# A hybrid RWKV-7 and Conformer layer on one core: the convolution's LayerNorm in two steps, two gate pairs kept in SBUF, and an order for the first squares

## The chip, the core and the metric

The kernel runs on one core of a Trainium2 chip. The time is that of one execution on the device in microseconds, the median of several. The core has five engines, each of which works through its own list of instructions in a fixed order and waits by semaphores for the others: TensorE (PE) for matrix products, VectorE (DVE) and ScalarE (ACT) for elementwise work, GpSimd (POOL), and SyncE (SP), which issues most transfers. PE loads weights (PEld) beside a running product. Products land in PSUM, which has eight banks; everything else is kept in SBUF in named tiles with a fixed number of buffers.

## What is computed

One layer of a decoder over a prompt of 2048 tokens (width 1024) and eight sample tokens. The convolution branch and the merge, which the change touches, are in the reference:

```python
h = rms_norm(x, norm_pre_g)
proj = jnp.einsum('btd,dn->btn', h, w_in)
...
u = u_in[..., :D_CONV] * jax.nn.sigmoid(u_in[..., D_CONV:])
c = lax.conv_general_dilated(buf, conv_w[:, None, :], ...) + conv_b      # 31 taps per channel
cm = jnp.mean(cf, axis=-1, keepdims=True)
cv = jnp.mean(jnp.square(cf - cm), axis=-1, keepdims=True)
cn = (cf - cm) * lax.rsqrt(cv + LN_EPS) * ln_c_g + ln_c_b
o_c = jax.nn.silu(cn) * jax.nn.silu(z_c)
branch_c = o_c @ w_branch_c
merged = jax.nn.sigmoid(g_r) * branch_r + jax.nn.sigmoid(g_c) * branch_c
y = x + rms_norm(merged @ w_out, norm_post_g)
```

The other branch is the RWKV-7 recurrence over 16 heads, done in chunks of 64 tokens, which needs a triangular solve per chunk.

## The kernel before

The prompt is cut into four blocks of 512 tokens; everything is kept transposed, channels on the partitions and tokens along the row. Each product of `gemm` makes 128 output channels of a block from 8 tiles of the input with three passes (the high part of both factors, and the two mixed terms), so 24 matmuls of 512 columns. In block 0 and in the merges of block 2, where the sample tokens ride along, a product takes two banks and twice as many matmuls of half the width. The products rotate through three PSUM banks, `pg`.

A block's loop goes over eight units j (two heads each). In each, `unit_b(j)` runs the recurrence's scan and `unit_a(j + 1)` prepares the next unit, of which the solve is a long chain of small DVE operations (lines 600 to 611); `unit_in(j + 2)` makes four products. Behind them come the fill steps of a table, one string for each j: `u` makes a channel tile of the gated linear unit (`glu`), whose 31 taps then run on DVE in small portions (`pull`), a digit makes a pair of output gates (`gate`), `n` is the LayerNorm over the 512 channels (`conv_norm`), `z` and `Z` multiply two channel tiles each with the gate of the convolution (`conv_gate`). Then `conv_split`, the next block's first products, eight merges (`merge`, two products each) and the output product (`stage_out`).

`conv_norm` adds the four channel tiles, sums over the partitions with a product with a constant matrix (`stat` with `avg_c`, line 767), subtracts, squares, sums the squares the same way (line 776), and scales. `gate` stores its sigmoids in DRAM (line 1010, issued by ACT) and `merge` loads the two rows that it needs (lines 1026 and 1027, issued by SP), both through the tag `x`, which has two buffers. `tmp` has four buffers and serves the norm, the gates of the convolution, and `unit_a`. `stage_first` normalizes the first block: it squares eight tiles of the prompt, adds and sums them, and beside it makes the sample rows' norm (`rms`).

The order on each engine is made at build time by a scheduler that goes by the order in which instructions are traced and by a model of when their inputs are ready. `later(n)` lets what it holds count as n instructions later; `behind` and `issue_after` place instructions on their engine's list behind a given one, without a wait for its end.

Of the kernel before, what the change touches and what calls it, by code (L numbers as in the profile page):

```python
# [15 lines left out]
RJ = 3  # L16
GE, HPO, HPA = 4, 0, 0
LI = 1000
LN = 200
HP = 550  # L20
HPW, HPS, HPG, HPU, HPZ = HP, HP, HP, HP, HP
LN_EXP_SET = 6
# [4 lines left out]
def rwkv7_conformer_step(  # L27
# [6 lines left out]
    nc = tc.nc  # L34
# [264 lines left out]
        return tiles  # L299

    FT, MTP, GTP, GM = 6, 6, 6, (3, 6)
    FILL0 = ("u0", "u1", "u2", "u3", "4n", "5", "6", "7zZ")
    FILL1 = ("0", "1", "2n", "z", "Z", "3", "4", "567")
    FILL2 = ("", "", "0n", "z", "Z", "1", "", "234567")
    UT = 2
    PARK = 2
    DW = {SB - 1: (2, 1, 0, 1, 0, 1, 0, 0), SB: (0, 0, 1, 0, 1, 0, 1, 1)}
    PASSES = ((0, 0), (0, 1), (1, 0))

    def gemm(specs):  # L310


        views = []
        for src, key, rhs, w2 in specs:
            ws = wload(src, key)
            v = View()
            if w2:
                outs = [(pgt()[:, 0:PW], slice(0, PW)), (pgt()[:, 0:w2], slice(PW, PW + w2))]
                v.parts = [(o[:, 0:HB], slice(i * HB, i * HB + HB)) for i, (o, _) in enumerate(outs)]
                v.s = [o[:, HB:PW] for o, sl in outs if sl.stop - sl.start == PW]  # L320
            else:
                outs = [(pgt(), slice(0, BS))]
                v.parts = outs
            n = 4 * len(ws)
            for o, sl in outs:
                for kt in range(n):
                    for pi, (wp, ap) in enumerate(PASSES):
                        mm(o, ws[kt // 4][:, wp, kt % 4, :], rhs(kt, ap)[:, sl],
                           start=(kt == 0 and pi == 0), stop=(kt == n - 1 and pi == 2))
            views.append(v)  # L330
        return views

# [57 lines left out]
    def stage_first():  # L390

        n1 = NS + 1
        xts = [new([128, 2, BS], tag) for tag in ("x", "x", "orr", "orr")]
        xts = [xts[kt // 2][:, kt % 2] for kt in range(KT)]
        for kt in range(KT):
            nc.sync.dma_start(out=xts[kt], in_=x_cols[kt, :, 0:BS])
        xs = new([128, D], "orr")
        nc.sync.dma_start(out=xs[0:NS], in_=x_sample[:, 0, :])
        nc.sync.dma_start(out=xs[NS:n1], in_=x_prompt[0, T - 1:T, :])
        gb = new([128, D], "orr")  # L400
        nc.sync.dma_start(out=gb[0:n1], in_=norm_pre_g[0:1, :].to_broadcast([n1, D]))
        sh = new([128, D], "orr")
        nc.sync.dma_start(out=sh[0:NS], in_=state_shift[0])
        rstd = rms(xs, n1, "orr", [128, D])
        h9 = new([128, D], "orr")
        stt(h9[0:n1], xs[0:n1], rstd[0:n1], gb[0:n1], ALU.mult, ALU.mult)
        with later(LI):
            nc.scalar.dma_start(out=nshift_s[0], in_=h9[0:NS])
            nc.scalar.dma_start(out=nshift_p[0], in_=h9[NS:n1])
        ps = pa()  # L410
        psv = ps[:, 0:KT * 2 * NS].rearrange("p (k i s) -> p k i s", k=KT, i=2)
        for kt in range(KT):
            for i, src in enumerate((h9, sh)):
                nc.tensor.transpose(out=psv[:, kt, i, :], in_=src[0:NS, kt * 128:kt * 128 + 128],
                                    identity=ident[0:NS, 0:NS])
        rb = new([128, BS], "tmp")
        for kt in range(KT):
            sq = rb if kt == 0 else new([128, BS], "tmp")
            act(sq, xts[kt], AF.Square)
            if kt:  # L420
                tt(rb, rb, sq, ALU.add)
        rsqrt(rb, stat(pyt, avg_c, rb), eps_rms, scale=float(DC) / D)
        ht = [new([128, 2, WX], "ht", F32R) for _ in range(KT)]
        for kt in range(KT):
            stt(xts[kt], xts[kt], pv("npre", kt), rb, ALU.mult, ALU.mult)
            split(wide(True, ht[kt][:, 0]), wide(True, ht[kt][:, 1]), two(True, xts[kt]))
            hv = ht[kt].rearrange("p h (i t) -> p h i t", i=2)[:, :, :, HB:PW]
            split(hv[:, 0], hv[:, 1], psv[:, kt])
        return ht
# [330 lines left out]
        return acc  # L760

    def conv_norm(b, cs):
        sm = new([128, BS], "tmp")
        tt(sm, cs[0], cs[1], ALU.add)
        for ct in range(2, CT):
            tt(sm, sm, cs[ct], ALU.add)
        ps = stat(pgt, avg_c, sm)
        for ct in range(CT):
            tt(cs[ct], cs[ct], ps, ALU.subtract)
        sm = new([128, BS], "tmp")  # L770
        act(sm, cs[0], AF.Square)
        for ct in range(1, CT):
            sq = new([128, BS], "tmp")
            act(sq, cs[ct], AF.Square)
            tt(sm, sm, sq, ALU.add)
        ps = stat(pgt, avg_c, sm)
        rs = new([128, BS], "tmp")
        rsqrt(rs, ps, eps_ln)
        for ct in range(CT):
            mul(cs[ct], cs[ct], rs)  # L780
            s1 = new([128, BS], "tmp")
            sigmoid(s1, cs[ct], nscale=nlng[:, ct:ct + 1], nbias=nlnb[:, ct:ct + 1])
            act(cs[ct], cs[ct], AF.Identity, scale=pv("lng", ct), bias=pv("lnb", ct))
            mul(cs[ct], cs[ct], s1)

    def conv_gate(b, ht, cs, c0):
        for i, z in enumerate(gemm([hspec(b, ht, N_SHIFT + 2 * DC + (c0 + i) * 128) for i in range(2)])):
            ct = c0 + i
            s2 = new([128, BS], "tmp")
            with tc.high_priority(HPZ):  # L790
                sigmoid_v(s2, z)
                for ps, sl in z.parts:
                    mul(s2[:, sl], s2[:, sl], ps)
                if b == 0:
                    vcp(sconv[:, 2 * CT + ct, :], z.s[0])
            mul(cs[ct], cs[ct], s2)

    def conv_split(b, cs):
        wd = b == SB
# [195 lines left out]
    G0 = N_SHIFT + 3 * DC  # L995
    gates = [[dram.tile([128, 2, BS], F32, name=f"gate{b}_{i}") for i in range(KT)] for b in range(NB)]

    def gate(b, ht, i0):

        vs = gemm([hspec(b, ht, G0 + (i0 + i) * 128) for i in range(2)])  # L1000
# [6 lines left out]
                    vcp(gate_s[:, i0 + i, :], v.s[0])  # L1007
        act(s, s, AF.Ln, bias=1.0)
        act(s, s, AF.Exp, scale=-1.0)
        nc.scalar.dma_start(out=gates[b][i0 // 2], in_=s)  # L1010

    def merge_prep(b, orr):
        if b == SB:
# [5 lines left out]
    def merge(b, m, orr, oc):  # L1019
# [1 line left out]
        w2 = HB if wd else None  # L1021
        br, bcv = gemm([(w_branch_r[m], ("br", m), lambda kt, part: orr[kt][:, part, :], w2),
                        (w_branch_c[m], ("bc", m), lambda kt, part: oc[kt][part], w2)])
        sc = new([128, 2, BS], "x")
        s, c = sc[:, 0], sc[:, 1]
        nc.sync.dma_start(out=s, in_=gates[b][m // 2][:, m % 2])
        nc.sync.dma_start(out=c, in_=gates[b][(KT + m) // 2][:, m % 2])
        for t, v in ((s, br), (c, bcv)):
            for ps, sl in v.parts:
                mul(t[:, sl], t[:, sl], ps)  # L1030
# [100 lines left out]
    def fill(b, ht, cs, what):  # L1131
# [3 lines left out]
        elif what == "n":  # L1135
            while taps:
                pull(1)
            with later(LN):
                conv_norm(b, cs)
        elif what in "zZ":  # L1140
            conv_gate(b, ht, cs, 2 * (what == "Z"))
        else:
            gate(b, ht, 2 * int(what))
# [129 lines left out]
```

## Time and profile before

| | us |
|---|---|
| three runs | 2832.56, 2832.91, 2835.99 |
| median | 2832.91 |
| profiled execution | 2830.14 |
| its span | 2828.4 |
| PE busy | 2680.2 |
| DVE busy | 1965.0 |
| ACT busy | 1318.7 |
| stores of gates, 512 KB each | 32 |
| loads of gates, 256 KB each | 64 |

Rows of a timeline give the start, the duration, the engine, the line, the operation, what it writes and reads with the tile's name, and the count of equal instructions that were drawn together. Brackets hold the time for which the engine stood idle before, and what ended that. Line numbers are often those of a helper: 101 is an operation on two tiles, 107 one with a scalar besides, 95 an activation, 113 a matmul.

### The profile page before, as it was taken

How to read it: one execution, taken by the hardware profiler on the slowest of the kernel's cores; microseconds unless marked ns; L12 is line 12 of the kernel's file. 1: busy time of each engine (PE TensorE's matmuls, PEld its weight loads, DVE VectorE, ACT ScalarE, POOL GpSimd, SP SyncE). 2: the span in 40 equal slices, each digit the busy share in tenths (PEclk: the TensorE clock that was granted, in tenths of full speed). 3: DMA queues.
4: the chain of work that ended last, by engine and by line, in shares of the span. 5: the costliest groups of instructions: out<-in, count | busy, mean ns of one | idle time of the engine just before them, and what ended most of it. 6: DMA issues, size and time to landing. Idle time of an engine off the chain costs nothing.

```text
span 2828.4 us, 55917 instructions
## 1 busy us (share of the span) xinstructions
PE 2680.2 (95%) x22800; PEld 2129.1 (75%) x22800; DVE 1965.0 (69%) x4560; ACT 1318.7 (47%) x2783; POOL 16.1 (1%) x61
## 2 busy tenths in 40 slices
PE   6999898999999989999999998999999997999988
PEld 6888887878877767777887766777797765777777
DVE  5789898677877667667568667676665767765522
ACT  5555556662344464555113556555312455545511
POOL 0000000000000000000000000000000000000000
PEclk9999999999999999999999999999999998999999
DMA  5555754547964334254665335344475422332474
GB/s 197 202 172 189 209 179 137 182 160 249 316 240 136 105 122 136 100 168 160 215 239 202 106 103 151 116 138 162 160 237 205 156 88 71 108 117 98 135 275 161
DMA packets 153107, 466.91 MB, mean 165 GB/s; under 512 B 19281, under 2 KB 24642, under 8 KB 152843
## 3 DMA queue, kind: packets, MB, share of 16 engines
q1 hardware_dynamic: 145745, 437.55, 46.3%
q10 hardware_dynamic: 7106, 25.79, 2.5%
q8 instruction: 179, 2.93, 0.4%
q14 instruction: 77, 0.63, 0.1%
HBM read 350.41 MB, written 113.35 MB: 164 GB/s over the span
## 4 chain that ended last, share of the span: by engine, by line
PE 53%; DVE 29%; ACT 13%; issue 3%; DMA 2%; SPq 0%; POOL 0%; DVEq 0%; ACTq 0%; POOLq 0%
PE pg L113 34%; PE pa L113 7%; DVE gd L101 5%; DVE zr L605 5%; PE pc L113 4%; PE py L113 4%; DVE zr L107 3%; DVE et L107 3%; ACT sc L95 2%; PE pb L113 2%; DVE raw L107 2%; ACT zbuf L95 2%; ACT xv L95 1%; DVE w L101 1%; ACT tmp L95 1%
## 5 line engine op out<-in xcount | busy, mean ns | idle before, releaser
L113 PE MATMUL pg<-ht,w 128*128 128x512 f32 (+1 forms) x7200 | 1518.6, 362 | 15.1 <-DVE sraw L110 5.3
L113 PEld LDWEIGHTS pg<-ht,w 128*128 128x128 f32 x7200 | 1163.2, 189 | 255.5 <-issue 59.8
L107 DVE SCALAR_TENSOR_TENSOR et<-u,cw,et 128x512 f32<-128x512 f32 x480 | 359.4, 749 | 6.7
L95 ACT ACTIVATE raw<-pg,omm 128x512 f32<-128x512 f32 (+1 forms) x155 | 92.9, 602 | 208.9 <-PE pg L113 201.4
L95 ACT ACTIVATE tmp<-tmp 128x512 f32<-128x512 f32 (+1 forms) x305 | 185.0, 625 | 9.0 <-DVE tmp L526 3.2
L101 DVE TENSOR_TENSOR gd<-zr,gp 128x8 f32<-128x8 f32 (+14 forms) x480 | 179.7, 374 | 11.7
L113 PE MATMUL pg<-orr,w 128*128 128x512 f32 (+2 forms) x960 | 185.0, 349 | 0.0
L605 DVE TENSOR_REDUCE zr<-gd 128x2 f32<-128x8 f32 (+14 forms) x480 | 176.6, 368 | 11.7
L113 PEld LDWEIGHTS pg<-orr,w 128*128 128x128 f32 x960 | 155.2, 188 | 25.1
L95 ACT ACTIVATE w<-wraw 128x512 fp32r<-128x512 f32 x162 | 101.3, 627 | 117.8 <-PE pg L113 75.4
L698 DVE TENSOR_SCALAR xs<-pc,dk 128x64 f32<-128x64 f32 x224 | 63.5, 284 | 111.6 <-PE pc L113 109.3
L95 ACT ACTIVATE sc<-pa 64x256 f32<-64x256 f32 (+1 forms) x192 | 72.9, 380 | 136.4 <-PE pb L113 133.1
L101 DVE TENSOR_TENSOR w<-wraw,w 128x512 fp32r<-128x512 f32 x162 | 111.0, 687 | 32.2 <-ACT w L95 31.5
L107 DVE SCALAR_TENSOR_TENSOR raw<-pg,prm,raw 128x511 f32<-128x511 f32 (+1 forms) x185 | 104.3, 574 | 29.9 <-ACT raw L95 29.3
L107 DVE SCALAR_TENSOR_TENSOR zr<-zr,sub 128x5 f32<-128x5 f32 (+7 forms) x512 | 115.7, 226 | 13.3
L95 ACT ACTIVATE gd<-sc 32x128 f32<-32x128 f32 x256 | 78.4, 306 | 92.2 <-DVE sc L101 89.6
L101 DVE TENSOR_TENSOR x<-x,pg 128x512 f32<-128x512 f32 (+1 forms) x80 | 46.2, 578 | 94.6 <-PE pg L113 56.5
L113 PE MATMUL pa<-ar,bk 64*64 64x128 f32 x2048 | 105.7, 285 | 5.6 <-DVE sc L101 3.2
L113 PEld LDWEIGHTS pa<-ar,bk 64*64 64x64 f32 x2048 | 81.3, 136 | 39.2 <-DVE bk L101 15.2
L101 DVE TENSOR_TENSOR sc<-pa,maskw 128x512 f32<-128x512 f32 x128 | 82.7, 685 | 30.8 <-PE pa L113 30.7
L101 DVE TENSOR_TENSOR keep<-pa,raw 128x512 f32<-128x512 f32 x32 | 22.1, 692 | 113.9 <-PE pa L113 113.9
L113 PE MATMUL pg<-xv,w 128*128 128x512 f32 (+2 forms) x320 | 89.8, 354 | 8.8 <-DVE x L101 8.8
(360 smaller groups left out, 3654.3 us busy)
## 6 DMA issues: line engine op xcount, KB each, us to landing
w<-kept_in SPq DMA_DIRECT2D x366, 512.0 KB, 3.3
kept_in<-w SPq DMA_DIRECT2D x122, 512.0 KB, 4.0
wraw<-in_w_in_dram SPq DMA_DIRECT2D x122, 256.0 KB, 3.2
w<-kept_br SPq DMA_DIRECT2D x48, 512.0 KB, 4.1
w<-kept_out SPq DMA_DIRECT2D x40, 512.0 KB, 4.3
gate<-x ACTq DMA_DIRECT2D x32, 512.0 KB, 4.9
x<-gate SPq DMA_DIRECT2D x64, 256.0 KB, 3.9
w<-kept_bc SPq DMA_DIRECT2D x24, 512.0 KB, 3.5
```

The costliest lines, as they stand in the source:

```text
L95: return nc.scalar.activation(out=out, in_=in_, func=func, scale=scale, bias=bias, **kw)
L101: return nc.vector.tensor_tensor(out=out, in0=a, in1=b, op=op)
L107: return nc.vector.scalar_tensor_tensor(out=out, in0=a, scalar=s, in1=b, op0=op0, op1=op1)
L113: return nc.tensor.matmul(out=out, lhsT=lhsT, rhs=rhs, start=start, stop=stop, **kw)
L605: nc.vector.tensor_reduce(out=zr[:, 0:n, t:t + 2], in_=pr[:, 0:n, :, 0:w], axis=AX.X, op=ALU.add)
L698: nc.vector.tensor_scalar(out=state[:, j, :] if c == NC - 1 else xs[:, c + 1, :], in0=pu[:, c * C:c * C + C], scalar1=dk[:, c:c + 1], scal ...
```

## The change

The second half of `conv_norm`, from the squares on, becomes a function of its own, `conv_scale`, and is called in `conv_gate` for the first pair, behind the product for `z`. Both sums over the partitions are placed on PE's list behind the last product that was traced before them. The lowered priority of the norm falls away. The multiplication with the gates' `s2` follows behind `conv_scale`.

The order of the gates in the fill tables is moved on by one, so that pairs 0 and 4 are last. These two stay in their `x` buffers and are read from there by merges 0 and 1; they are neither stored nor loaded.

In `stage_first` the squares of the prompt's tiles are traced ahead of the sample rows' norm, and that norm is placed on ACT's list behind the last of the squares.

```diff
-LN = 200
...
-    FILL0 = ("u0", "u1", "u2", "u3", "4n", "5", "6", "7zZ")
-    FILL1 = ("0", "1", "2n", "z", "Z", "3", "4", "567")
-    FILL2 = ("", "", "0n", "z", "Z", "1", "", "234567")
+    FILL0 = ("u1", "u2", "u3", "u5", "6n", "7", "0", "4zZ")
+    FILL1 = ("1", "2", "3n", "z", "Z", "5", "6", "704")
+    FILL2 = ("", "", "1n", "z", "Z", "2", "", "356704")
...
-                        mm(o, ws[kt // 4][:, wp, kt % 4, :], rhs(kt, ap)[:, sl],
-                           start=(kt == 0 and pi == 0), stop=(kt == n - 1 and pi == 2))
+                        done[0] = mm(o, ws[kt // 4][:, wp, kt % 4, :], rhs(kt, ap)[:, sl],
+                                     start=(kt == 0 and pi == 0), stop=(kt == n - 1 and pi == 2))
...
-        rstd = rms(xs, n1, "orr", [128, D])
+        rb = new([128, BS], "tmp")
+        for kt in range(KT):
+            sq = rb if kt == 0 else new([128, BS], "tmp")
+            last = act(sq, xts[kt], AF.Square)
+            if kt:
+                tt(rb, rb, sq, ALU.add)
+        with behind(last.ins):
+            rstd = rms(xs, n1, "orr", [128, D])
...
     def conv_norm(b, cs):
+
         sm = new([128, BS], "tmp")
         tt(sm, cs[0], cs[1], ALU.add)
         for ct in range(2, CT):
             tt(sm, sm, cs[ct], ALU.add)
-        ps = stat(pgt, avg_c, sm)
+        with tc.issue_after(done[0].ins):
+            ps = stat(pgt, avg_c, sm)
         for ct in range(CT):
             tt(cs[ct], cs[ct], ps, ALU.subtract)
+
+    def conv_scale(b, cs):
+
         sm = new([128, BS], "tmp")
         act(sm, cs[0], AF.Square)
         for ct in range(1, CT):
             sq = new([128, BS], "tmp")
             act(sq, cs[ct], AF.Square)
             tt(sm, sm, sq, ALU.add)
-        ps = stat(pgt, avg_c, sm)
+        with tc.issue_after(done[0].ins):
+            ps = stat(pgt, avg_c, sm)
...
     def conv_gate(b, ht, cs, c0):
-        for i, z in enumerate(gemm([hspec(b, ht, N_SHIFT + 2 * DC + (c0 + i) * 128) for i in range(2)])):
+        vs = gemm([hspec(b, ht, N_SHIFT + 2 * DC + (c0 + i) * 128) for i in range(2)])
+        s2s = []
+        for i, z in enumerate(vs):
             ct = c0 + i
             s2 = new([128, BS], "tmp")
+            s2s.append(s2)
...
-            mul(cs[ct], cs[ct], s2)
+        if c0 == 0:
+            conv_scale(b, cs)
+        for i, s2 in enumerate(s2s):
+            mul(cs[c0 + i], cs[c0 + i], s2)
...
-        nc.scalar.dma_start(out=gates[b][i0 // 2], in_=s)
+        if i0 in (0, KT):
+            held[i0] = s
+        else:
+            nc.scalar.dma_start(out=gates[b][i0 // 2], in_=s)
...
-        sc = new([128, 2, BS], "x")
-        s, c = sc[:, 0], sc[:, 1]
-        nc.sync.dma_start(out=s, in_=gates[b][m // 2][:, m % 2])
-        nc.sync.dma_start(out=c, in_=gates[b][(KT + m) // 2][:, m % 2])
+        if m < 2:
+            s, c = held[0][:, m], held[KT][:, m]
+        else:
+            sc = new([128, 2, BS], "x")
+            s, c = sc[:, 0], sc[:, 1]
+            nc.sync.dma_start(out=s, in_=gates[b][m // 2][:, m % 2])
+            nc.sync.dma_start(out=c, in_=gates[b][(KT + m) // 2][:, m % 2])
...
-            with later(LN):
-                conv_norm(b, cs)
+            conv_norm(b, cs)
```

## Rows read from the trace of the kernel before

**Rows 1.** The page's first part: busy time of each engine, its share of the span, and instructions.

```profile
PE 2680.2 (95%) x22800; PEld 2129.1 (75%) x22800; DVE 1965.0 (69%) x4560; ACT 1318.7 (47%) x2783; POOL 16.1 (1%) x61
```

**Rows 2.** The waits of PE by what ended them, over the whole span: microseconds in total, times, the longest.

```profile
PE pg L113 <- DVE tmp L101: 26.1, 6, 7.0
PE pb L113 <- DVE gd L609: 20.2, 22, 4.1
...
PE pg L113 <- DVE x L101: 8.8, 1, 8.8
```

**Rows 3.** The timeline of PE at the sums of the norm that wait: the second sum of blocks 0, 1 and 2, and the first of block 3.

```profile
470.64 2.08 PE L113 MATMUL pg<-tmp,avg_c 128*128 128x512 f32 x2 [7.00 <-DVE tmp L101]
...
1048.00 2.08 PE L113 MATMUL pg<-tmp,avg_c 128*128 128x512 f32 x2 [4.93 <-DVE tmp L101]
...
1723.70 2.08 PE L113 MATMUL pg<-tmp,avg_c 128*128 128x512 f32 x2 [6.61 <-DVE tmp L101]
...
2390.59 2.08 PE L113 MATMUL pg<-tmp,avg_c 128*128 128x512 f32 x2 [5.74 <-DVE tmp L101]
```

**Rows 4.** Busy time in five stretches, the first four from the end of a wait of rows 3, the last from that of rows 10: bounds, length, busy us (instructions) of PE, PEld, DVE, ACT and POOL, the mean granted clock of TensorE as a share of full speed, the DMA engines' busy share, GB/s.

```profile
470.60:485.20 14.60, 14.30 (x95) 12.88 (x95) 14.21 (x38) 10.66 (x19) 0.00 (x0) 0.88 0.19 55
1048.00:1065.20 17.20, 16.73 (x65) 12.53 (x66) 16.57 (x44) 12.43 (x20) 0.00 (x0) 0.91 0.38 122
1723.70:1745.10 21.40, 21.24 (x84) 16.14 (x86) 20.77 (x55) 12.43 (x20) 0.00 (x0) 0.93 0.58 163
2390.60:2404.40 13.80, 11.41 (x139) 8.51 (x140) 12.40 (x29) 6.22 (x16) 0.00 (x0) 0.56 0.01 1
2721.10:2732.20 11.10, 11.06 (x37) 8.88 (x38) 4.73 (x7) 1.26 (x2) 0.00 (x0) 0.74 0.45 142
```

**Rows 5.** The timeline where the solve ends that runs beside the second sum, in blocks 1 and 2: the transpose with which DVE hands it over, and PE's first product with it.

```profile
1064.68 0.43 DVE L609 STREAM_TRANSPOSE gd<-zr 128x256 f32<-128x256 f32 x1
1065.17 0.69 PE L113 MATMUL pb<-gd,sc 32*32 32x32 f32 x32 [0.47 <-DVE carry L110]
...
1745.06 0.69 PE L113 MATMUL pb<-gd,sc 32*32 32x32 f32 x32 [0.16 <-DVE gd L609]
```

**Rows 6.** Groups of DVE's instructions from 1042 to 1065.2, the solve of block 1 beside the second sum: count, busy us, mean ns, idle us before them.

```profile
L101 DVE TENSOR_TENSOR et<-et,tmp 128x512 f32<-128x512 f32 x8 | 5.5, 684 | 0.0
...
L101 DVE TENSOR_TENSOR tmp<-tmp 128x512 f32<-128x512 f32 x3 | 2.1, 688 | 0.0
```

**Rows 7.** The timeline of DVE at the first and the last operation of a solve with nothing of the norm in it, in block 3.

```profile
2342.75 0.14 DVE L110 COPY sub<-gp 128x16 f32<-128x16 f32 x1
...
2359.36 0.45 DVE L609 STREAM_TRANSPOSE gd<-zr 128x256 f32<-128x256 f32 x1
```

**Rows 8.** The instructions on the tile `et`, which holds the convolution's channels, over the whole span: the squares, the first step of the sigmoid, and the affine step, with the shortest, median and longest duration in ns, and the first and last start.

```profile
L95 ACT ACTIVATE tmp<-et x16: 612/625/631, 464.9 to 2395.6; 128x512 f32<-128x512 f32 x16
L95 ACT ACTIVATE tmp<-et,nlnb,nlng x16: 802/807/819, 475.8 to 2412.7; 128x512 f32<-128x512 f32 x16
L95 ACT ACTIVATE et<-et,prm x16: 799/804/809, 478.1 to 2415.7; 128x512 f32<-128x512 f32 x16
```

**Rows 9.** Busy time in two stretches at the end of block 0, with the columns of rows 4: the last products of block 0, and the last scan up to block 1's products.

```profile
585.00:611.00 26.00, 23.83 (x253) 22.70 (x248) 23.50 (x69) 12.37 (x27) 0.00 (x0) 1.00 0.69 225
611.00:637.00 26.00, 23.66 (x290) 16.09 (x291) 17.67 (x39) 15.60 (x37) 0.34 (x1) 0.93 0.27 85
```

**Rows 10.** The timeline around the first merges of block 3: the last store of gates, the first load, and what waits for it.

```profile
2698.64 0.33 ACTq L1010 DMA_DIRECT2D gate<-x  x1
...
2714.71 0.75 SPq L1026 DMA_DIRECT2D x<-gate  x1
...
2720.39 1.38 DVE L101 TENSOR_TENSOR x<-x,pg 128x512 f32<-128x512 f32 x2 [34.99 <-DMA x<-gate]
2721.14 0.80 PE L113 MATMUL pg<-xv,w 128*128 128x512 f32 x1 [8.82 <-DVE x L101]
```

**Rows 11.** The timeline of a merge of block 2: the start of its first products, a load of gates behind the merge before it, and the start of what follows its products.

```profile
2098.06 5.91 PE L113 MATMUL pg<-orr,w 128*128 128x264 f32 x48
...
2101.59 0.32 SPq L1026 DMA_DIRECT2D x<-gate  x1
...
2106.69 11.29 PE L113 MATMUL pg<-ht,w 128*128 128x512 f32 x48
```

**Rows 12.** The issues of transfers from 2690 to 2760: count, size, and the median time from the issue to the landing in us.

```profile
x<-gate SPq DMA_DIRECT2D x14, 256.0 KB, 3.6
```

**Rows 13.** The timeline of the head: the square of the sample rows, the transposes of the rows, the last square of a tile, the split of the fourth weight tile, the sum over the partitions, and the first product.

```profile
13.21 1.05 ACT L95 ACTIVATE orr<-orr 9x1024 f32<-9x1024 f32 x1 [11.13 <-DMA orr<-in_x_sample_dram]
...
17.54 1.87 PE L414 MATMUL pa<-ident,orr 8*128 8x8 f32 x16 [13.05 <-DVE orr L107]
...
20.84 0.62 ACT L95 ACTIVATE tmp<-orr 128x512 f32<-128x512 f32 x1
...
22.51 0.63 ACT L95 ACTIVATE w<-wraw 128x512 fp32r<-128x512 f32 x1 [1.05 <-DMA wraw<-in_w_in_dram]
...
23.79 2.04 PE L113 MATMUL py<-tmp,avg_c 128*128 128x512 f32 x2 [4.38 <-DVE tmp L101]
...
28.72 1.03 PE L113 MATMUL pg<-ht,w 128*128 128x264 f32 x3 [2.89 <-ACT ht L95]
```

**Rows 14.** The issues of transfers from 7.2 to 8.02, the last two tiles of the first block: count, size, and the median time to landing in us.

```profile
orr<-in_x_cols_dram SPq DMA_DIRECT2D x2, 256.0 KB, 4.2
```

More of the change, by code (lines that the diff above doesn't have):

```diff
@@ L308, in rwkv7_conformer_step @@
     PASSES = ((0, 0), (0, 1), (1, 0))
+    done = [None]
     def gemm(specs):
@@ L415, in stage_first @@
                                     identity=ident[0:NS, 0:NS])
[L416 to L421, printed above, removed]
         rsqrt(rb, stat(pyt, avg_c, rb), eps_rms, scale=float(DC) / D)
@@ L996, in rwkv7_conformer_step @@
     gates = [[dram.tile([128, 2, BS], F32, name=f"gate{b}_{i}") for i in range(KT)] for b in range(NB)]
+    held = {}
     def gate(b, ht, i0):
```

## The prediction

> **What bounds the kernel now.** I read five views, in this order. The busy table first: TensorE (PE) works 95% of the span and no other engine passes 75% [rows 1], so a gain has to come from PE's gaps, 148 us in all. Then PE's waits by releaser: sums that VectorE (DVE) writes into `tmp`, 26.1 us in six waits; the end of the triangular solve, 20.2 us in 22 waits; one wait of 8.8 us for a gate product [rows 2]. Then the PE timeline at those places: four of the six are `conv_norm`'s channel sums, 7.00, 4.93 and 6.61 us for the second sum (of squares) of blocks 0, 1 and 2, and 5.74 us for the first sum (the mean) of block 3, 24.28 us together [rows 3]. Then the granted clock behind them, and last DVE's own work in those stretches. The head, before the first product, is read by itself.
>
> **Norm: what PE can get back.** Behind each wait the clock stood for a while on its lower level of 1.2 GHz. A stretch of length L with mean granted clock c lost (1-c)L: 0.12 x 14.6 = 1.75 us, 0.09 x 17.2 = 1.55, 0.07 x 21.4 = 1.5 [rows 4]. In block 3 that is 0.44 x 13.8 = 6.1, but PE is busy only 11.41 of 13.8 us there and partly waits; I count 3. So PE's side is 8.75, 6.5, 8.1 and 8.7 us, 32 together.
>
> It doesn't get all of that, and this is the step to watch. At the end of the solve in which the stall lies, PE has no slack: DVE's transpose ends the solve at 1065.11 and PE's next small product starts at 1065.17; in block 2 PE waits 0.16 us for it [rows 5]. So DVE was the late one over the whole stretch, and a PE that doesn't stop at the sum arrives early and waits at the solve's end, unless DVE gets faster too. The Trainium skill, in Perfetto Trace Analysis, Identifying the Most-Contended Engine, says that TensorE's busy share is no good measure of its limit and that the weight loads' share is: 75% here against 95%, so by that page PE isn't the limit and the wait comes up elsewhere, which is rival 1, 2819 us against the forecast's 2799. The trace bears it out at the solves' ends and not elsewhere.
>
> DVE does get faster there, because the change takes the second half of the norm out of this solve: eight scalings, 5.5 us, and three adds, 2.1 us, 7.6 us between 1042 and 1065; a solve without them runs from 2342.75 to 2359.81, 17.1 us, against some 23 [rows 6, 7]. The gain of a block is the smaller side: 7.6, 6.5, 7.6 and 7.6, 29.3 us. (In block 3 the mean's seven operations of 0.7 also leave the chain that PE waits for, as they lose their lowered priority. In blocks 0 to 2 they only come earlier: between 0 and 4.8 us if they push a solve, which I take as 0, since no first sum waits there.)
>
> **Norm: where the work goes.** The second half is now traced behind the product for `z`, one unit later in blocks 1 to 3. Its sum is issued behind 48 products, and the squares that feed it have been computable since the step before, so I cost its wait at 0; if DVE is behind, it is again up to 7 us [rows 3]. Its 7.6 us on DVE lie in another solve or in a scan step. That can be anything from 0 (gaps) to 7.6 (all of it in a chain for which PE waits); the nearest row is the wait at the solves' ends, 20.2 / 22 = 0.9 us each [rows 2], which says that the scheduler mostly lays enough products beside them. I take 3 us in each of the three blocks, 9 us. Queued behind the pinned sum on PE are the next unit's products; ACT's `rsqrt` waits for it. The new order of the fill steps by itself moves equal products past each other: 0.
>
> Block 0 is worse. Its `z` product stands in the last unit, so the second half falls onto the block's end: on ACT four squares at 0.625, `rsqrt` as two such, four rounds of 0.807 + 2 x 0.625 + 0.804, 15.2 us, and on DVE 7.6 us [rows 6, 8]. ACT has room (12.37 busy of 26 us, then 15.60 of 26), DVE hardly (23.50 of 26, then 17.67) [rows 9], and the next block's activations queue behind it on both engines, with PE waiting for them. Bounds 0 and 15.2; DVE's load decides, and I take 5 us of its 7.6. Norm in all: 29.3 - 9 - 5 = 15.3 us.
>
> **Gates held on chip.** It removes two gate pairs of eight in each block, so 8 of 32 stores and 16 of 64 loads. That is worth something only where a load is late: block 3. The load for the first merge stands behind weight loads on SP's queue, is issued at 2714.71 although the last store left at 2698.64, and DVE gets it at 2720.39; PE has then waited 8.82 us [rows 10], and (1-0.74) x 11.1 = 2.9 us more go to the clock [rows 4]. Gone: 11.7 us, nearly all of which counts, as PE works without gaps from there to its last merge. What is late next is merge 2: both buffers of tag `x` are held until merge 1 has read them, so its loads can't run ahead. In blocks of one bank per product it has to be consumed only after its own products and two thirds of the next merge's, 14 us behind merge 1's. In block 2, with two banks per product, PE needs the first bank back after 60 of 72 parts of 8.63 us, 7.2 us; there a load is issued 3.53 us behind the products before it and takes 3.6, 7.1 us [rows 11, 12]: no slack. Between 0 and 4 us (another weight load ahead of it on SP costs some 3), I take 1. Net 10.7.
>
> **Head.** ACT's first work is the sample norm's square, which waits 11.13 us for its row, to 13.21; the squares of the tiles stand behind it, the last at 20.84; the sum runs at 23.79 and the first product at 28.72, 4.93 later [rows 13]. Issued first, the squares follow the tiles: the last two land 4.2 us behind their issue before 8.02 [rows 14], so by about 12; last square to 12.6, one add 0.7, then the same 4.93: 18.2. The sample rows need 13.21 to 19.41 (17.54 + 1.87) as it is, with squares in between; now weight splits of the same length lie in between. Copying them out, the first product comes at about 20.2, when the fourth weight tile, at 22.51 today, has moved up as well. The gain is 8.5 us; 4.4 if the transposes stay ahead of the sum on PE (19.4 + 4.93), at best 10.5. I count 8.0. SP's queue isn't changed; behind the pinned norm on ACT stand the weight splits.
>
> **Sum.** 15.3 + 10.7 + 8.0 = 34 us off the profiled execution, 2830.1 us (a span of 2828.4 and 1.7 around it): 2796. The median of the runs, 2832.9, is 2.8 above it: 2799 us, 1.2% faster. About 0.2%, 5.7 us, is what a measurement here can tell from no change. Its own range, not all terms at their ends at once: 2789 to 2811.
>
> **Rivals.**
> 1. *The norm's waits come back at the solve's end.* DVE stays the late engine: norm 0, block 0's end still 5. 10.7 + 8 - 5 = 13.7 us, 2819. For: the missing slack [rows 5]. Against: 7.6 us leave those solves [rows 6, 7].
> 2. *All of it passes.* The work finds gaps: 32 + 11.7 + 9 = 52.7 us, 2780. For: ACT's idle half [rows 9].
> 3. *Slower: `z`'s buffers starve the next unit.* `conv_gate` now holds two of the four `tmp` buffers from `z`'s sigmoid until the scaled channels are ready; `conv_scale` needs two for itself and the next unit's first part four. The hold is as long as the ACT work above, 15 us, and where PE has no products for it, it costs up to that in each block. From 8.5 us per block it eats the 34 us; at 13 it gives +18, 2851. For: in block 3 the norm and a unit share these buffers just where PE idles most [rows 4]. Against: the unit's second part, traced between, needs none of this tag.
> 4. *The gains cancel:* rival 3 at 8 us a block, within 0.2% of 2833.
>
> **How the numbers follow.** Forecast 0.50, rival 1 0.20, rival 2 0.15, rival 3 0.09, rival 4 0.06. Faster 0.85, same 0.06, slower 0.09. The range leaves out rivals 3 and 4 and the lower edge of rival 2: 2777 to 2826.
>
> **What would show it.** Right: no wait of PE over 2 us for the channel sums, the granted clock at 1.00 there, the first product by about 20 us, 24 stores and 48 loads of gates, no wait in merge 0 of block 3. The sum of the waits at the solves' ends decides: 20 to 29 us is the forecast, 45 is rival 1. Block 0's end shows its 5 us in a later first product of block 1. Wrong: a unit's first part that starts late behind `z` (rival 3), or a first product at 24 us (the transposes).

## The result and the profile after

The changed kernel takes 2821.07 us (median of 6 runs, 2811.94 to 2825.32) against 2836.93 us for the kernel before (6 runs, 2832.56 to 2839.83, the three already shown among them): a ratio of 0.9946, 95% interval 0.9934 to 0.9958. So it is 0.54% or 15.9 us faster, where 34 us off were forecast. The direction is as predicted and the time lies in the range (2777 to 2826), close to the 2819 of rival 1.

The profiled execution took 2822.38 us (span 2820.7, mean granted clock 0.984). Its busy line, to set beside [rows 1]:

```profile
PE 2690.1 (95%) x22800; PEld 2138.2 (76%) x22800; DVE 1961.8 (70%) x4560; ACT 1321.7 (47%) x2783; POOL 16.1 (1%) x61
```

PE's gaps, span less busy time, fell from 148.2 to 130.6 us, 17.6 us. But PE's busy time rose by 9.9 us for the same 22800 matmuls, as the clock stood lower (0.984 against 0.987). One can take this further. The span less the gaps is PE's busy time; less (1 - clock) x span, with c for the granted clock, it is nearly the same in the eight profiles of the table (last column). The clock is on record to three digits, so the last two columns are good to 1.4 us.

| kernel | span | gaps of PE | (1 - c) x span | rest |
|---|---|---|---|---|
| before | 2828.4 | 148.2 | 36.8 | 2643.4 |
| after | 2820.7 | 130.6 | 45.1 | 2645.0 |
| after, repeated (r_after) | 2813.8 | 130.3 | 39.4 | 2644.1 |
| norm change alone (e_norm) | 2831.0 | 141.0 | 45.3 | 2644.7 |
| all but the norm (e_nonorm) | 2815.1 | 137.1 | 31.0 | 2647.0 |
| after, five `tmp` (e_tmp5) | 2801.4 | 120.7 | 30.8 | 2649.9 |
| the same, repeated (r_tmp5) | 2809.0 | 122.8 | 39.3 | 2646.9 |
| after, one tile for the gates (e_own) | 2808.1 | 123.7 | 42.1 | 2642.3 |

The gaps belong to the kernel (130.6 and 130.3 in two executions of the same program); the clock's part differs by some 6 us between the two. A single profile is therefore read by its gaps, and times by medians. In the mean over all runs of a series, though, the clock's part goes with the kernel too: 46.0 and 43.4 us in the two series of the changed kernel, 33.8 in `e_nonorm`, 33.7 and 33.0 with five `tmp`, 37.2 in `e_own`, 38.4 to 41.2 in the kernel before beside them.

The waits of PE by what ended them, changed kernel (total, times, longest; beside [rows 2]; line numbers have moved by a few):

```profile
PE pb L112 <- DVE gd L611: 20.5, 20, 4.1
...
PE pa L112 <- DVE sc L100: 10.4, 18, 1.6
PE pa L112 <- DVE bk L100: 8.8, 8, 3.3
PE pg L112 <- DVE tmp L100: 8.5, 4, 3.5
PE pb L112 <- ACT gp L94: 7.9, 6, 2.8
...
PE pg L112 <- DVE x L100: 1.2, 1, 1.2
```

and three of the same rows in the kernel before:

```profile
PE pa L113 <- DVE sc L101: 6.3, 12, 1.6
...
PE pb L113 <- ACT gp L95: 2.1, 2, 1.8
PE pa L113 <- DVE bk L101: 2.0, 6, 0.4
```

Three things are to be seen. The merge's wait is gone (8.8 to 1.2). The channel sums' waits fell by 17.6 us, from 26.1 [rows 2] to 8.5. And three waits of a unit's first part and solve rose: `bk` from 2.0 to 8.8, `sc` from 6.3 to 10.4, `gp` from 2.1 to 7.9, together 16.7 us. With the old norm and everything else changed (`e_nonorm`) these three stand at 2.0, 5.8 and 2.1, so it is the norm change that raised them. Of what the sums gave back, nearly as much came up in the unit. The solves' ends (`gd`), on which the forecast wanted the case decided, did not move.

PE's timeline at the sums and at two of the new waits in the changed kernel; the first two are second sums, the fourth is the first sum of block 3:

```profile
589.53 2.07 PE L112 MATMUL pg<-tmp,avg_c 128*128 128x512 f32 x2 [3.52 <-DVE tmp L100]
...
1106.83 1.72 PE L112 MATMUL pg<-tmp,avg_c 128*128 128x512 f32 x2 [1.02 <-DVE tmp L100]
...
1771.27 0.44 PE L112 MATMUL pa<-ar,bk 64*64 64x128 f32 x4 [1.92 <-DVE bk L100]
...
2387.67 2.07 PE L112 MATMUL pg<-tmp,avg_c 128*128 128x512 f32 x2 [1.01 <-DVE tmp L100]
...
2453.01 0.69 PE L112 MATMUL pa<-ar,bk 64*64 64x128 f32 x4 [3.31 <-DVE bk L100]
```

Busy time around the two new waits (columns of [rows 4]): over these 14 us the clock is at 0.63 and 0.51, against 0.56 to 0.93 in the stretches behind the old sums.

```profile
1770.00:1784.00 14.00, 10.28 (x139) 8.76 (x139) 10.78 (x25) 8.51 (x18) 0.00 (x0) 0.63 0.12 39
2452.00:2466.00 14.00, 10.54 (x134) 8.57 (x135) 11.42 (x28) 8.27 (x18) 0.00 (x0) 0.51 0.03 10
```

At the same products in `e_nonorm`, where no wait for `bk` is longer than 0.4 us, the clock is 1.00:

```profile
1769.00:1783.00 14.00, 13.66 (x168) 10.28 (x167) 11.39 (x31) 7.48 (x16) 0.00 (x0) 1.00 0.32 111
2453.00:2467.00 14.00, 13.59 (x165) 10.57 (x164) 11.40 (x30) 5.65 (x14) 0.00 (x0) 1.00 0.24 82
```

Where DVE's part went is read from the first copy of a solve (`sub`) and the transpose that ends it. Units 3 and 4 of block 3 in the changed kernel:

```profile
2404.57 0.14 DVE L109 COPY sub<-gp 128x16 f32<-128x16 f32 x1
2421.71 0.45 DVE L611 STREAM_TRANSPOSE gd<-zr 128x256 f32<-128x256 f32 x1
...
2463.28 0.14 DVE L109 COPY sub<-gp 128x16 f32<-128x16 f32 x1
2487.32 0.45 DVE L611 STREAM_TRANSPOSE gd<-zr 128x256 f32<-128x256 f32 x1
```

and in `e_nonorm`:

```profile
2400.04 0.14 DVE L109 COPY sub<-gp 128x16 f32<-128x16 f32 x1
2422.27 0.45 DVE L611 STREAM_TRANSPOSE gd<-zr 128x256 f32<-128x256 f32 x1
...
2463.55 0.14 DVE L109 COPY sub<-gp 128x16 f32<-128x16 f32 x1
2481.23 0.45 DVE L611 STREAM_TRANSPOSE gd<-zr 128x256 f32<-128x256 f32 x1
```

In the changed kernel unit 3 needs 17.6 us (to the transpose's end), unit 4 24.5. With the old norm they need 22.7 and 18.1. In blocks 1 and 2 it is the same: unit 3 goes from 23.1 and 31.0 to 18.5 and 26.2, unit 4 from 25.0 and 19.1 to 31.2 and 23.4, and the last unit of block 0 from 22.0 to 27.6. The second half of the norm left one solve and went into the next one, nearly whole.

### The profile page after: what moved, and what is told of

It reads as the page before. It is cut to its first block, busy times and chain, and to the rows that moved or that the text cites. A ratio compares the mean times of both kernels' runs of the same rounds, so it can differ in the third digit from the quotient of the medians.

```text
span 2820.7 us, 55887 instructions
## 1 busy us (share of the span) xinstructions
PE 2690.1 (95%) x22800; PEld 2138.2 (76%) x22800; DVE 1961.8 (70%) x4560; ACT 1321.7 (47%) x2783; POOL 16.1 (1%) x61
## 4 chain that ended last, share of the span: by engine, by line
PE 54%; DVE 27%; ACT 13%; DMA 4%; issue 2%; SPq 0%; POOL 0%; DVEq 0%; ACTq 0%; POOLq 0%
PE pg L112 35%; PE pa L112 8%; DVE gd L100 5%; DVE zr L607 5%; PE pc L112 4%; PE py L112 4%; DVE zr L106 3%; DVE et L106 2%; PE pb L112 2%; ACT sc L94 2%; DVE raw L106 2%; ACT tmp L94 2%; ACT zbuf L94 2%; DMA wraw<-in_w_in_dram 1%; DVE w L100 1%
## 5 line engine op out<-in xcount | busy, mean ns | idle before, releaser
L112 PEld LDWEIGHTS pa<-ar,bk 64*64 64x64 f32 x2048 | 82.6, 138 | 45.6 <-DVE bk L100 19.2
L100 DVE TENSOR_TENSOR keep<-pa,raw 128x512 f32<-128x512 f32 x32 | 22.1, 692 | 118.3 <-PE pa L112 118.3
L112 PEld LDWEIGHTS pc<-xs,aw 64*64 64x64 f32 x1024 | 51.1, 131 | 60.3 <-DVE xs L700 38.3
```

Of the source, the lines that this page charges most:

```text
L100: return nc.vector.tensor_tensor(out=out, in0=a, in1=b, op=op)
L112: return nc.tensor.matmul(out=out, lhsT=lhsT, rhs=rhs, start=start, stop=stop, **kw)
```

## The experiments

Each group below was timed beside the same runs of the kernel before; differences in us are those of the medians to before, ratios carry 95% intervals.

**The parts by themselves.** The theory from the two traces (A): the norm change moves DVE's work from a solve into the next and is worth about nothing; gates and head make the gain. The rival (B): the forecast's norm term holds and something else lost 19 us. `e_head` is the kernel before with the new `stage_first`, `e_held` with the gates' order and hold, `e_norm` with the two-step norm, `e_nonorm` the changed kernel with the old norm:

```diff
-            conv_norm(b, cs)
+            with later(200):
+                conv_norm(b, cs)      # whole again, sums not pinned, conv_gate as before
```

> The kernel before with the change of the head alone (squares of the tiles ahead of the sample rows' norm). Theory A (the norm's second half only moved from one solve into the next, so the norm change is worth about 0): 3 to 5 us faster than before, as the first solve ends 4.9 us earlier in the changed kernel; first product at 25.3 us. Theory B (the norm change gains its 15 us and something else lost 19 us): 0 to 3 us faster, because the head's gain is eaten behind it.

> The kernel before with the gates alone (the moved order of the gate pairs, pairs 0 and 4 held on chip). Theory A: 9 to 13 us faster, all of it behind the last solve (172.6 to about 162 us from there to the end). Theory B: 0 to 5 us faster.

> The kernel before with the norm change alone (two steps, sums pinned, no lowered priority). Theory A: within 4 us of before: the solve that loses the second half ends 2 to 5 us earlier, the next unit's solve in blocks 1 to 3 takes 6 to 7 us longer, block 0's end 4 us. Theory B: 12 to 18 us faster.

> The changed kernel with the norm as it was before (whole, with the lowered priority, sums not pinned): head and gates only. Theory A: 12 to 17 us faster than before, as fast as the whole change. Theory B: 0 to 5 us faster than before, so 10 us and more slower than the whole change.

| | ratio to before | us |
|---|---|---|
| e_head | 0.9985 [0.9977, 0.9994] | -3.8 |
| e_held | 0.9951 [0.9939, 0.9964] | -12.3 |
| e_norm | 0.9987 [0.9977, 0.9996] | -4.6 |
| e_nonorm | 0.9941 [0.9928, 0.9955] | -15.4 |

A's numbers nearly hold: without the norm change the kernel is as fast as with it. Alone the norm is worth 4.6 us, 0.6 more than A allowed and at most 6.5 by its interval, against 15.3 forecast. The two get to the same time by different ways: `e_nonorm` has 6.5 us more of PE's gaps than the changed kernel (137.1 and 130.6), and in the mean over its runs 10 to 12 us less lower clock.

**Where the norm's gain goes.** Theory A blames the scalings in the next solve; then taking them out of it must pay. Two ways: put them behind the solve, or leave them out. The third kernel tests the prediction's rival 3, the fourth the head.

```diff
+        solved[0] = nc.vector.transpose(out=zv[:, :, 32:64], in_=zt)      # e_pin
...
-            mul(cs[ct], cs[ct], rs)
+            with tc.issue_after(solved[0].ins):
+                mul(cs[ct], cs[ct], rs)
```

```diff
-            mul(cs[ct], cs[ct], rs)                                       # e_noscale
...
-            mul(cs[ct], cs[ct], s1)
```

```diff
-tmp=4                                                                     # e_tmp5
+tmp=5
```

```diff
+            with behind(*(g for g in gate_in if g)):    # e_head2: gate_in[0] is the last square
                 split(w[:, 0], w[:, 1], raw)
```

> The changed kernel; the scalings of conv_scale are placed on DVE's list behind the transpose that ends the solve of the unit traced before. Theory A (the second half's DVE work lies in the next unit's solve, where DVE is the late engine): the solves of unit 4 in blocks 1 to 3 shrink from 31.2, 23.4 and 24.5 us to about 25, 19 and 18, that of unit 7 of block 0 from 27.6 to 22, and the kernel is 10 to 20 us faster than the changed one, 26 to 36 faster than before. Rival (the scan behind the solve has no room on DVE either, or the clock decides): the distance from a solve's end to the next solve's start grows by as much, and the time stays within 5 us of the changed kernel.

> The changed kernel without the eight multiplications of conv_scale on DVE (by the rsqrt and by the sigmoid), so the convolution's branch is neither scaled by its deviation nor gated by its own sigmoid; all else is as it was. Theory A: 5.5 us of DVE less in the same four solves, 12 to 22 us faster than the changed kernel. Rival (products or the clock set the time there): within 5 us of it. Against e_pin it tells what the multiplications still cost in their new place.

> The changed kernel with five buffers of tag tmp instead of four. If the gates' two tiles that are held through conv_scale starve the next unit (the prediction's third rival, at a small price), it is 4 to 12 us faster than the changed kernel. Theory A: within 4 us of it, as the work on DVE stays where it is.

> The changed kernel with the first weights' splits placed behind the last of the tiles' squares on ACT and DVE. If the split that stands ahead of the last two squares, waiting 3.4 us for its weight tile, is what kept the first product at 25.3 us: first product at 19 to 21 us, 3 to 6 us faster than the changed kernel. If the transposes or the fourth weight tile hold it: first product at 23 us or later, within 2 us of it. Part of the gain may be lost again in block 0, as with the first part of it.

| | ratio to before | us |
|---|---|---|
| e_pin | 0.9943 [0.9930, 0.9955] | -15.8 |
| e_noscale | 0.9909 [0.9895, 0.9923] | -24.7 |
| e_tmp5 | 0.9904 [0.9888, 0.9920] | -27.8 |
| e_head2 | 0.9927 [0.9915, 0.9940] | -18.9 |

`e_pin` did to the solves what was expected: unit 4 takes 26.6, 18.3 and 19.2 us, unit 7 of block 0 19.7. And it gained nothing. These rows are the end of unit 4's solve in block 3 and the first activation of the unit behind it, first in `e_pin`:

```profile
2480.11 0.45 DVE L612 STREAM_TRANSPOSE gd<-zr 128x256 f32<-128x256 f32 x1
2504.90 0.69 ACT L94 ACTIVATE tmp<-pa,nw 128x512 f32<-128x512 f32 x1 [2.25 <-PE pa L112]
```

and in the changed kernel:

```profile
2487.32 0.45 DVE L611 STREAM_TRANSPOSE gd<-zr 128x256 f32<-128x256 f32 x1
2502.52 0.69 ACT L94 ACTIVATE tmp<-pa,nw 128x512 f32<-128x512 f32 x1 [2.64 <-PE pa L112]
```

The unit behind begins 24.3 us after the solve instead of 14.8: the work went on to the next place where something waits for it. So theory A is right about where the work lies and wrong that the solve is what makes it dear. Leaving the multiplications out brings 9 us. That is not the price of these operations alone: nothing waits for the `rsqrt` of the second sum any more either, and the gates' tiles are free sooner. But the fifth buffer, which takes away no work, brings 12, three times what A allowed. Buffers of `tmp` are short, then, which is the ground of rival 3 (put at 9 in 100), at a smaller price than it was given; whether it is the gates' hold that makes them short, the next two groups ask.

**Is it the hold?** The next four were to tell apart the gates' hold of two `tmp` tiles (theory C) from a buffer that helps any form of the kernel. `e_nonorm_tmp5` is the old norm with five; `e_order` calls `conv_scale` ahead of `z`'s products, so that the scaling comes before the gates' tiles are taken; `e_pin_tmp5` and `e_tmp5_head2` combine earlier edits.

```diff
     def conv_gate(b, ht, cs, c0):                                         # e_order
+        if c0 == 0:
+            conv_scale(b, cs)
         vs = gemm(...)
...
-        if c0 == 0:
-            conv_scale(b, cs)
```

> Head and gates with the norm as it was before, and five buffers of tag tmp: the fourth corner beside the changed kernel (new norm, four buffers), the one with five buffers, and the one without the norm change. Theory C (the norm change is good for 10 us and more, but only where the two tiles that the gates now hold don't take buffers from the next unit or block): no faster than with four buffers, 12 to 18 us faster than before, so 10 us and more slower than the new norm with five. Rival (a fifth buffer helps any form of this kernel): 24 to 30 us faster than before, as fast as the new norm with five.

> The changed kernel with conv_scale traced ahead of z's products instead of behind them, four buffers: nothing of the gates is held through the scaling, and the pinned second sum comes some 48 products earlier. Theory C: 6 to 14 us faster than the changed kernel, the end of block 0 (from its last solve to the next block's first) some 4 us shorter. Rival (the scalings on DVE are the whole price): within 4 us of the changed kernel.

> The changed kernel with the scalings placed behind the end of the next solve, and five buffers. With four buffers this placing brought nothing: the solves became 5 us shorter and the unit behind started its first activation 24.3 us behind the solve instead of 15. Theory C: with a fifth buffer that start comes back by 4 us or more, and the kernel is 0 to 8 us faster than the one with five buffers alone. Rival (it is the chain of scalings and sigmoids itself that stands ahead of the next unit on ACT and DVE): the start stays at 24 us, and the kernel is slower than with five buffers alone by 5 to 15 us.

> The changed kernel with five buffers of tmp and the first weights' splits placed behind the last square: the two edits that helped, together. If they add up: 2800 to 2805 us, 16 to 20 us faster than the changed kernel. If the head's gain is lost in block 0: no faster than five buffers alone.

| | ratio to before | us |
|---|---|---|
| e_nonorm_tmp5 | 0.9932 [0.9919, 0.9944] | -19.9 |
| e_order | 1.0021 [1.0012, 1.0030] | +4.5 |
| e_pin_tmp5 | 0.9917 [0.9905, 0.9930] | -24.5 |
| e_tmp5_head2 | 0.9907 [0.9891, 0.9922] | -29.7 |

The old norm gains 4.5 us from the fifth buffer (from -15.4 to -19.9), the new one 12 (10 when it was repeated). That lies between what theory C and its rival expected. The difference of 5.5 to 7.5 us is no larger than the intervals of the four ratios allow, so that most of the gain is particular to the new norm is likely by this, not shown. `e_pin_tmp5` went against theory C: the start behind the solve stayed at 24.2 to 24.3 us, so there it is the chain of scalings and sigmoids itself that stands ahead of the next unit, not the buffer. The kernel is 3 us slower than with five buffers alone, within the intervals.

`e_order` was a clear miss, 20 us slower than the changed kernel. It takes the hold away but sets the squares ahead of the unit's first part, so it doesn't test the hold by itself; PE then waits for `bk` 5.4 to 6.0 us in each of the four blocks (first line of PE's waits in `e_order`):

```profile
PE pa L112 <- DVE bk L100: 27.3, 11, 6.0
```

**Who needs the tile.** `r_after` and `r_tmp5` time the two kernels again, side by side; `e_own` gives one tile of its own to the second gate tile and to nobody else, `e_rb` gives it to the row with which the next block's first stage begins.

```diff
-            s2 = new([128, BS], "tmp")
+            s2 = new([128, BS], "zs" if i else "tmp")      # e_own
...
-        rb = new([128, BS], "tmp")
+        rb = new([128, BS], "rbt")                         # e_rb, in stage_a
```

> The changed kernel again, beside the three others. Both theories: a ratio to before of 0.993 to 0.996.

> The changed kernel with five buffers of tmp again. If the effect of the fifth buffer is real: 8 us and more faster than the changed kernel of the same call. If it was the granted clock of that call: within 4 us of it.

> Four buffers of tmp, and a tile of its own for the second of the two gate tiles of z and of Z: the fifth tile goes to nobody else. If the gates' hold is what takes the buffer: as fast as with five buffers of tmp (within 4 us), with fewer waits of PE for sc and gp (18.3 us together in the changed kernel, 11.7 with five buffers). If it is someone else's need: as fast as the changed kernel.

> Four buffers of tmp, and a tile of its own for the row of rms factors with which a block begins. If that row's load, issued at 610.2 us in the changed kernel and at 595.3 with five buffers, is what costs at the blocks' ends: 5 to 12 us faster than the changed kernel, the way from block 0's last solve to block 1's first activation down from 203.3 to about 200 us. If not: within 3 us of the changed kernel.

| | ratio to before | us |
|---|---|---|
| r_after | 0.9942 [0.9929, 0.9956] | -17.2 |
| r_tmp5 | 0.9905 [0.9892, 0.9919] | -27.2 |
| e_own | 0.9911 [0.9898, 0.9925] | -24.7 |
| e_rb | 0.9961 [0.9949, 0.9974] | -11.0 |

The effect repeats (10 us), and the one tile for the gates alone gives three quarters of it or all, within the intervals. The waits for `sc` and `gp` in `e_own`, which were 10.4 and 7.9:

```profile
PE pa L112 <- DVE sc L100: 4.7, 12, 1.3
PE pb L112 <- ACT gp L94: 4.3, 4, 1.8
```

What the hold does to the order is seen in block 3, from the unit's first activation (`tmp<-pa,nw`) over the first and second gate tile to the second sum. Changed kernel:

```profile
2437.43 0.69 ACT L94 ACTIVATE tmp<-pa,nw 128x512 f32<-128x512 f32 x1 [3.18 <-PE pa L112]
2444.65 0.58 ACT L94 ACTIVATE tmp<-pg 128x512 f32<-128x512 f32 x1
2452.27 0.68 DVE L100 TENSOR_TENSOR bk<-tmp 128x512 f32<-128x512 f32 x1
...
2453.05 0.60 ACT L94 ACTIVATE tmp<-pg 128x512 f32<-128x512 f32 x1 [0.45 <-DVE bk L100]
...
2464.84 1.47 PE L112 MATMUL pg<-tmp,avg_c 128*128 128x512 f32 x2
```

With the tile of its own (`e_own`):

```profile
2427.16 0.69 ACT L94 ACTIVATE tmp<-pa,nw 128x512 f32<-128x512 f32 x1 [3.18 <-PE pa L112]
2434.38 0.58 ACT L94 ACTIVATE tmp<-pg 128x512 f32<-128x512 f32 x1
2439.43 0.60 ACT L94 ACTIVATE zs<-pg 128x512 f32<-128x512 f32 x1 [0.95 <-PE pg L112]
...
2447.52 2.08 PE L112 MATMUL pg<-tmp,avg_c 128*128 128x512 f32 x2 [0.89 <-DVE tmp L100]
```

The first gate tile comes 7.2 us behind the unit's start in both. The second comes at 15.6 us in the changed kernel, released by the operation that writes `bk`, the last reader of one of the unit's own tiles; with its own tile it comes at 12.3. The second sum follows at 27.4 against 20.4. So squares and scalings slide by 7 us: the sum runs 1.6 us into the solve (which starts at 2463.28) instead of 9.4 us ahead of it (2456.88). The trace's wait is only 0.45 us long, on ACT: the order of the list had already been made for the missing buffer.

This is not yet the price. From the start of unit 3's solve in block 3 to that of unit 5's it is 123.5 and 123.4 us in the two profiles of the changed kernel and 123.0 in `e_own`: the solve starts later there and is shorter. The largest share of the gain lies in block 0, where both halves of `z` and the scaling fall into the last unit. The first solve of block 1 starts, in the changed kernel and in `e_own`, at

```profile
839.72 0.14 DVE L109 COPY sub<-gp 128x16 f32<-128x16 f32 x1
...
834.97 0.14 DVE L109 COPY sub<-gp 128x16 f32<-128x16 f32 x1
```

(841.56 in the repeated run of the changed kernel, 836.70 and 832.73 with five buffers). Which waits in block 0 make it up was not taken apart. The waits for `bk` don't belong to the hold: 8.8 us in the changed kernel, 8.9 in `e_own`, 9.0 and 8.8 with five buffers. Why `bk` is late with the new norm stays open.

The Trainium skill, in Perfetto Trace Analysis, Optimization Strategy (under Identifying Performance Opportunities), says that a gap which keeps coming back on the engine that should be saturated can mean that SBUF has no room for the next tile. Here the count of buffers bears it out, with the 10 us of `r_tmp5` as the price, but not the trace's gaps: none of PE's waits in the changed kernel is shown as one for a free buffer.

`e_rb` is no faster than `r_after`, so the blocks' first row isn't what needs the tile. Why it is 6 us slower stays open.

## Why the prediction was right and where it failed

**Bound by PE's gaps: right only with the clock beside them.** The last column of the first table holds within 8 us over profiles that are up to 30 us apart; over all eighteen profiles of the case it runs from 2638.6 (`e_order`, clock 0.982) to 2650.8 (`e_tmp5_head2`, 0.989). The gaps alone don't give the time: `e_nonorm` has 6.5 us more of them than the changed kernel and is as fast (2820.08 and 2821.07 us).

**Gates, 10.7 us: right.** `e_held` measures 12.3 us (10 to 17 by its interval). Of the gates there are 24 stores and 48 loads left. What was late next is merge 2, as named, and at the price taken (1 us):

```profile
2734.61 0.69 DVE L100 TENSOR_TENSOR x<-x,pg 128x512 f32<-128x512 f32 x1 [14.15 <-DMA x<-gate]
...
2735.35 0.50 PE L112 MATMUL pg<-xv,w 128*128 128x512 f32 x1 [1.18 <-DVE x L100]
```

**Head, 8.0 us: the mechanism right, the size about twice what came.** The first product runs at 25.30 instead of 20.2 us, 3.4 earlier than [rows 13]. The prediction's bound for transposes ahead of the sum gave 24, but that isn't the cause: the transposes run behind the sum. ACT's and PE's timeline in the changed kernel:

```profile
10.22 1.28 ACT L94 ACTIVATE tmp<-orr 128x512 f32<-128x512 f32 x2
14.86 0.63 ACT L94 ACTIVATE w<-wraw 128x512 fp32r<-128x512 f32 x1 [3.36 <-DMA wraw<-in_w_in_dram]
15.40 1.13 ACT L94 ACTIVATE tmp<-orr 128x512 f32<-128x512 f32 x2
...
18.56 2.04 PE L112 MATMUL py<-tmp,avg_c 128*128 128x512 f32 x2 [14.25 <-DVE tmp L100]
...
20.86 1.87 PE L422 MATMUL pa<-ident,orr 8*128 8x8 f32 x16 [0.25 <-DVE orr L106]
...
25.30 1.03 PE L112 MATMUL pg<-ht,w 128*128 128x264 f32 x3 [2.58 <-ACT ht L94]
```

The last two squares stand behind the first weight's split on ACT's list, and that split waits 3.36 us for its transfer. "Last square to 12.6" is the step that failed: I had the splits only beside the sample rows' work. With the split behind the squares (`e_head2`) the rows are

```profile
12.79 0.63 ACT L94 ACTIVATE tmp<-orr 128x512 f32<-128x512 f32 x1 [0.67 <-DMA orr<-in_x_cols_dram]
...
14.29 2.05 PE L112 MATMUL py<-tmp,avg_c 128*128 128x512 f32 x2 [10.02 <-DVE tmp L100]
...
17.68 1.87 PE L425 MATMUL pa<-ident,orr 8*128 8x8 f32 x16 [1.34 <-DVE orr L106]
...
20.55 1.03 PE L112 MATMUL pg<-ht,w 128*128 128x264 f32 x3 [1.01 <-ACT ht L94]
```

and the first product comes at 20.55, as forecast. Its 4.8 us show as 3.0 in the medians (-18.9 against -15.9) and, with five buffers, as no more than 2.5, all within the intervals; that the two edits add up, as `e_tmp5_head2` was to show, did not come out.

**Norm, 15.3 us: the term that failed.** What PE gets back at the old sums was sized about rightly: the sums' waits fell by 17.6 us, and unit 3's solve is 4.6 to 5.1 us shorter, where 7.6 of DVE's work were taken out. The step that failed is "where the work goes", and in it a term that isn't there: the clock in the new place. To see it, cut each profile at the starts of its 32 solves. Four of the stretches hold the old sums that waited. The changes in PE's gaps and in (1 - clock) x length, in us, are:

| | gaps, those four | gaps elsewhere | clock, those four | clock elsewhere |
|---|---|---|---|---|
| before to `e_norm` | -20.5 | +13.2 | -10.1 | +16.9 |
| `e_nonorm` to after | -20.0 | +13.5 | -13.7 | +26.7 |
| `e_nonorm` to `r_after` | -22.1 | +15.3 | -8.3 | +15.9 |

The 9 + 5 us that the forecast took as the price are about what the gaps elsewhere grew by, 13 to 15 us. But it had counted the lower clock behind the old sums as a gain and put none against the new waits, and there 16 to 27 us came. Taken together, by these three rows 30 to 34 us were given back and 30 to 40 lost again. Not all of the clock's part is time, as idle time is in it, and it scatters between executions: 4.4 of the 26.7 us lie in a stretch of block 1 where the repeated run, with the same 2.6 us of gaps, has none.

How the new waits came about has three parts. First, "I take 3 us in each" for the second half in its new place: the next unit's solve is longer by 4.3 to 6.4 us, near the upper bound of 7.6 and not the middle. I had priced it by the wait at the solves' ends, 0.9 us each; but this row tells what PE loses with the solve as it is, not whether DVE has room in it for more. Second, "I cost its wait at 0": the second sum waits 3.5 us in block 0 and 1.0 in block 1. Third, the hold. Rival 3 was set aside because the unit's second part needs none of the tag; the tile is missed earlier, by the second gate tile itself, and it delays the squares. It costs some 7 to 12 us in all (`e_own`, `r_tmp5`, `e_tmp5`), not the 8 and more per block from which rival 3 was to decide. With the hold taken away the norm change is worth 7 to 8 us beside the other parts (-27.2 and -27.8 against -19.9, intervals that just touch), half of the 15.3.

Rival 1 had the right time (2819) by the wrong road: the waits at the solves' ends are 20.5 us, as in the forecast, not its 45. They came back at the next unit's first part, where neither the forecast nor rival 1 looked. The section of the Trainium skill that was cited with that rival (Perfetto Trace Analysis, Identifying the Most-Contended Engine) judges how close TensorE is to its roofline by MFU and by the weight loads' busy share. That PE isn't the limit was the prediction's own conclusion from it, and too strong: by that share PE, at 75% before and 76% after, still stands above DVE's 69 and 70%, and the time followed PE's gaps and clock.

**Sum.** Forecast 15.3 + 10.7 + 8.0 = 34; the parts alone give 4.6 + 12.3 + 3.8 = 20.7, together 15.9 to 17.2. The last 3 to 5 us are within the intervals.

A version that beats both kernels is the changed one with five buffers of `tmp`: 2807.24 and 2806.80 us in two sessions, ratios of 0.9904 and 0.9905.

## What to carry to other kernels

Work that is moved on an engine which is late in a chain is paid where it lands, unless that place has room on this engine; the wait that PE shows there today doesn't measure the room. New short waits are priced with the lower clock behind them, not by their length alone. A tile that is held longer is priced by counting who takes the tag's buffers while it is held, the holder's own second tile included; one more buffer is the cheapest test, since an order made for too few shows almost no wait. An instruction ordered early must also be looked at for what the scheduler puts between its parts: a split that waits for a transfer stopped the squares behind it.

## What the runs showed of the hardware

Two executions of the same program had the same gaps (130.6 and 130.3 us) and clocks of 0.984 and 0.986, some 6 us of span. Over the first six runs the changed kernel's time went roughly with its clock: 2811.94 us at 0.986, 2825.32 at 0.982. In `e_norm` the gaps shrank by 7.2 us while the clock took 8.5 more, so that its span (2831.0) wasn't below that of before: several short waits around small products went with a lower clock than the longest single wait. In the changed kernel, waits of 3.31, 0.64 and 1.01 us from 2453 on stand in 14 us at 0.51; the wait of 7.00 us in the kernel before was followed by 14.6 us at 0.88 [rows 4]; without these waits, around the same products, it was 1.00 (`e_nonorm`). Why it falls in some of these stretches in one execution and not in another wasn't settled.
